# Expert rounds of a two-layer backbone: TensorE in the order of the text, and weights asked for in the order of their reading

## The chip, the cores and the metric

The kernel runs on one core of one Trainium2 chip. The metric is the device time of one execution in microseconds (us); of a kernel's runs the median counts. The profile is one execution recorded by the hardware profiler; its times are counted from the start of its span.

## What is computed

Two layers over 512 latent tokens of width 1024 and 256 context tokens. Each layer mixes tokens (three head groups and an output projection) and then sends the latent tokens, in the first layer the context tokens too, through 16 experts. In the second layer, the last, only the 512 latent tokens go through them. Each expert picks the 64 tokens that score highest for it:

```python
def expert_choice_moe(h, w_router, w_gate, w_up, w_down):
    b, n, d = h.shape
    cap = EC_FACTOR * n // N_EXPERTS
    aff = jax.nn.softmax(jnp.einsum('bnd,de->bne', h, w_router).astype(jnp.float32), axis=-1)
    g, idx = lax.top_k(jnp.swapaxes(aff, 1, 2), cap)
    xs = jax.vmap(lambda hb, ib: hb[ib])(h, idx)
    hid = jax.nn.silu(jnp.einsum('becd,edf->becf', xs, w_gate)) * jnp.einsum('becd,edf->becf', xs, w_up)
    y = jnp.einsum('becf,efd->becd', hid, w_down) * g[..., None].astype(h.dtype)
    return jax.vmap(lambda yb, ib: jnp.zeros((n, d), h.dtype).at[ib.reshape(-1)].add(yb.reshape(-1, d)))(y, idx)
```

## The kernel before

All of it is fp32. The change lies in the expert part of the second layer (`if last:` in `layer`, from line 1710). The 16 experts go in eight rounds p = 0 to 7 of two experts, 128 gathered token rows a round. A round has these steps; the letters are those of the strings `M1` and `TL`, which say in what order the Python text lists them:

- **p**, `prep`: GpSimd gathers the 128 rows from DRAM with two indirect DMAs (L1541).
- **t**, `prep_t`: TensorE transposes them in eight pieces (L1554) into two PSUM tiles B; ScalarE (L1205) and VectorE (L1207) scale four pieces each into the tile `xs`.
- **g**, `gu`: 32 matmuls with the gate and up weights into one PSUM tile A, eight pieces of the width times gate and up times two experts. The experts are i = 0, 1; each uses 64 columns of the array (128*64 in the trace), and i = 0 and i = 1 follow each other in turn. Then ScalarE's Silu (L1573) and VectorE's product (L1574).
- **h**, `th_`: four transposes of that product (L1594), and a copy by ScalarE (L143).
- **d**, `dn`: 16 matmuls with the down weights into a tile A, again i = 0, 1 in turn; VectorE scales it twice by halves (L1613), ScalarE copies it rounded into `yh` (L143, 128x1024), VectorE makes the rest `yl` (L146), and the one-hot `oh` of the token numbers (L1617).
- **s**, `scat`: for four blocks of 128 tokens and two halves of the width a full 128-column matmul of `oh` with `yh` and one with `yl` into a tile B, which VectorE adds to the residual (L1673).

In the trace each 64-column matmul has two records, while a transpose and a matmul with `yh` or `yl` has one. All PE matmuls of `mm` have line L155. There are two PSUM tiles A and four B.

The weights are 1 MB loads by the SP queue (`wload`, L137): eight for gate and up of a round (`loads_gu`), four for down (`loads_d`), into a pool of 18 pages `pg`, two of the four down loads into the two buffers `aw`. A load waits for its page's last reader and for the load four before it; the queue keeps its order, so whatever stands behind a waiting load waits too. The last round's down weights come as halves of the width, for `dn_half` and `scat_half`, which send the output.

The scheduler of the framework sets the order on each engine: it takes the instructions by priority and by its own account of when they are ready, so TensorE's order need not be that of the text.

The order of the text before is `M1 = "tghpsd"` in a round (for step p: transposes and gate/up of p+1, `th_` of p, gather of p+2, scatter of p-1, down of p) for p up to 5; at p = 6 only h, s and d. Then `TL = "tsgh0123"`: transposes of 7, scatter of 6, gate/up of 7, `th_` of 7, the two down halves and the two scatter halves. The loads stand ahead of each round:

```python
                if p < 5:
                    loads_gu(p + 2)
                    loads_d(p + 1)
                elif p == 5:
                    loads_d(6)
                    loads_gu(7)
                    loads_d(7)
```

Of the kernel before, what the change touches and what calls it, by code (L numbers as in the profile page):

```python
# [64 lines left out]
DO1 = 1  # L65
# [30 lines left out]
def tile_hybrid_dit(ctx: ExitStack, tc: tile.TileContext, I: dict, out: bass.AP, mark=lambda s: None):  # L96
# [107 lines left out]

# [1 line left out]
    def ada_load(l, hf, u, w):  # L206
# [229 lines left out]
    def layer(l):  # L436
# [6 lines left out]

# [1 line left out]
        mark("ln1")  # L445
# [216 lines left out]
        else:  # L662
            ht(0, 0)
            consts()
            for k in range(8):
# [7 lines left out]
                fill(FL1[0] if k in FL1[5] else 0)  # L673
# [1 line left out]
        rv, sv = small(8), small(8)  # L675
# [70 lines left out]
        early(0)  # L746
# [1 line left out]
        mark("G3")  # L748
# [3 lines left out]
        for j in range(npair):  # L752
# [6 lines left out]
            split(t.rearrange("p (z e) -> p z e", z=2), fhv[:, i:i + 2], flv[:, i:i + 2])  # L759
# [1 line left out]
        early(1)  # L761
# [58 lines left out]

# [1 line left out]
        mark("sgu")  # L822
# [24 lines left out]

# [1 line left out]
        mark("four")  # L849
# [46 lines left out]

# [1 line left out]
        if WM:  # L898
# [118 lines left out]

# [1 line left out]
        mark("kv")  # L1019
# [77 lines left out]

# [1 line left out]
        units = [(0, h, a) for h in range(4) for a in range(LT)]  # L1099
# [91 lines left out]

# [1 line left out]
        mark("wo")  # L1193
# [328 lines left out]
        def loads_gu(p):  # L1522
            if p < 8:
                mark("moe")
                wpages(("w_gate", "w_up"), p, 8, (6, 7) if p == 0 and AW0[l] else ())

        def loads_d(p):
            if p < 8:
                mark("moe")
                wpages(("w_down",), p, 4, (2, 3) if p or not AW0[l] else (), last and p == 7)  # L1530

# [1 line left out]
        xc2 = xc_d.rearrange("n (h d) -> (n h) d", h=2)  # L1533

        def prep(s, p):
            ig = R[s][1]
            xg = t4()
            if s == 0:
                for i in range(2):
                    e = 2 * p + i  # L1540
                    pool.indirect_dma_start(out=xg[64 * i:64 * i + 64], out_offset=None, in_=xr_d[0],  # L1541
                                            in_offset=bass.IndirectOffsetOnAxis(ap=ig[:, e:e + 1], axis=0))
            else:
                for i in range(4):
                    e = 2 * p + i
                    pool.indirect_dma_start(out=xg[32 * i:32 * i + 32], out_offset=None, in_=xr_d[1],
                                            in_offset=bass.IndirectOffsetOnAxis(ap=ig[0:32, e:e + 1], axis=0))
            M["xg", s, p] = xg

        def prep_t(s, p):  # L1550
            xg = M["xg", s, p]
            t = [psB(), psB()]
            for k in (0, 4, 1, 5, 2, 6, 3, 7):
                pe.transpose(t[k // 4][:, (k % 4) * 128:(k % 4 + 1) * 128], xg[:, k::8], ident)  # L1554
            xs = t4()
            modT(s, t, lambda k: xs[:, k * 128:(k + 1) * 128], 128)
            M["xs", s, p] = xs
            if s:
                M["xs", s, p + 1] = xs
# [150 lines left out]
        if last:  # L1710
            if not DO1:
                loads_d(0)
            prep(0, 0)
            prep(0, 1)
            prep_t(0, 0)
            gu(0, 0)
            for p in range(7):
                if p < 5:
                    loads_gu(p + 2)
                    loads_d(p + 1)  # L1720
                elif p == 5:
                    loads_d(6)
                    loads_gu(7)
                    loads_d(7)
                for o in M1:
                    if o == "t" and p < 6:
                        prep_t(0, p + 1)
                    elif o == "p" and p < 6:
                        prep(0, p + 2)
                    elif o == "g" and p < 6:  # L1730
                        gu(0, p + 1)
                    elif o == "h":
                        th_(0, p)
                    elif o == "d":
                        dn(0, p)
                    elif o == "s" and p:
                        scat(p - 1)
            for o in TL:
                if o == "t":
                    prep_t(0, 7)  # L1740
                elif o == "s":
                    scat(6)
                elif o == "a":
                    scat(6, (0, 1))
                elif o == "b":
                    scat(6, (2, 3))
                elif o == "g":
                    gu(0, 7)
                elif o == "h":
                    th_(0, 7)  # L1750
                elif o in "01":
                    dn_half(7, int(o))
                elif o in "23":
                    scat_half(7, int(o) - 2)
        else:
# [136 lines left out]
```

## Time and profile before

| what | value |
|---|---|
| median of 3 runs | 1277.88 us (1272.85 to 1279.33) |
| span of the profiled execution | 1275.3 us |
| TensorE busy in the span | 1167.6 us (92%) |
| VectorE, ScalarE, GpSimd busy | 579.9, 379.5, 301.3 us |
| mean granted TensorE clock | 0.963 |
| read from HBM | 295.01 MB, 240 GB/s over the span |

For the profiled execution only the span is given, from its first to its last instruction; the median of the runs lies 2.5 us above it, and the span lies within the runs' range. The expert part of the second layer is the last fifth of the span, from about 1009 us on. In the trace section a line of a timeline gives start, length, engine, line, operation, operands and count, and in brackets the idle time before it with what ended it. Lengths of TensorE rows have modelled ends and reach some 0.1 us into the next row.

### The profile page before, as it was taken

Reading aid. Unit: us, or ns where it says so; the run is one execution under the profiler, and the core shown is the slowest. Engines: PE = TensorE matmul, PEld = TensorE weight load, DVE = VectorE, ACT = ScalarE, POOL = GpSimd, SP = SyncE. Lnnn points to the kernel's source line nnn. Section 1 sums busy time; section 2 is a strip of 40 time slices with the busy share of each in tenths; the row PEclk is TensorE's granted clock in tenths of the full one; section 3 lists DMA queues with packets and bytes.
Section 4 is the critical chain, followed back from the end, with each engine's and each line's share of the span. In section 5 each row is a group of like instructions: output and inputs, shape, how many; then the busy total and the mean of one; then the engine's idle time right before and its main releaser. Section 6 shows DMA issues by size and latency. Waiting matters only on the chain. (4 is left out here: it accounts for less than half of the span.)

```text
span 1275.3 us, 16762 instructions
## 1 busy us (share of the span) xinstructions
PE 1167.6 (92%) x6440; PEld 664.5 (52%) x6440; DVE 579.9 (45%) x1219; ACT 379.5 (30%) x921; POOL 301.3 (24%) x363
## 2 busy tenths in 40 slices
PE   4999998999998999999999899999999399999887
PEld 2668865777763333333333378756776133333332
DVE  5634567666563133222333545767654503322352
ACT  4424466554222111101111234565542011101110
POOL 2413553222222212111100434742232200000000
PEclk8999997999998999999999899999999599999999
DMA  9871462013189999999986542550256799999593
GB/s 339 300 267 40 170 221 92 1 61 138 54 327 324 342 323 320 364 327 360 347 327 230 161 163 75 186 197 1 100 185 271 275 401 407 386 396 396 217 396 131
DMA packets 74319, 306.59 MB, mean 240 GB/s; under 512 B 11008, under 2 KB 20480, under 8 KB 46080
## 3 DMA queue, kind: packets, MB, share of 16 engines
q1 hardware_dynamic: 67328, 285.59, 59.8%
q0 software_dynamic: 6048, 17.83, 4.9%
q10 hardware_dynamic: 864, 2.10, 0.4%
q8 instruction: 51, 0.84, 0.3%
q14 instruction: 28, 0.23, 0.0%
HBM read 295.01 MB, written 10.49 MB: 240 GB/s over the span
## 5 line engine op out<-in xcount | busy, mean ns | idle before, releaser
L155 PE MATMUL A<-pg,pg 128*128 128x512 f32 (+4 forms) x1440 | 354.7, 389 | 13.6 <-DVE pg L146 4.6
L155 PE MATMUL A<-pg,t 128*64 128x512 f32 x1248 | 301.9, 607 | 7.3 <-ACT t L143 3.5
L155 PEld LDWEIGHTS A<-pg,pg 128*128 128x128 f32 (+1 forms) x1440 | 255.8, 192 | 82.0 <-issue 22.1
L155 PEld LDWEIGHTS A<-pg,t 128*64 128x64 f32 x1248 | 89.6, 139 | 184.8 <-issue 163.2
L155 PE MATMUL B<-t,t 128*128 128x512 f32 x256 | 74.8, 424 | 16.4 <-ACT t L143 14.4
L1673 DVE TENSOR_TENSOR pg<-pg,B 128x512 f32<-128x512 f32 x112 | 69.5, 681 | 41.8 <-PE B L155 41.6
L143 ACT ACTIVATE pg<-B 64x256 fp32r<-64x256 f32 (+6 forms) x153 | 65.0, 445 | 73.4 <-PE B L155 37.2
L146 DVE TENSOR_TENSOR pg<-B,pg 128x512 fp32r<-128x512 f32 (+4 forms) x143 | 69.9, 500 | 34.7 <-ACT pg L143 27.7
L155 PE MATMUL B<-pg,t 128*32 128x512 f32 (+1 forms) x672 | 82.5, 609 | 1.6 <-ACT t L143 1.2
L1541 POOL DMA_INDIRECT t<-xr_d,ig x32 | 29.2, 913 | 229.7 <-PE B L155 120.5
L155 PE MATMUL B<-pg,pg 128*128 128x256 f32 (+6 forms) x552 | 81.8, 302 | 0.1
L155 PEld LDWEIGHTS B<-pg,pg 128*128 128x128 f32 x552 | 73.9, 189 | 11.9 <-issue 5.9
L1573 ACT ACTIVATE t<-A 128x512 f32<-128x512 f32 x16 | 9.6, 597 | 235.4 <-PE A L155 235.4
L1574 DVE TENSOR_TENSOR t<-t,A 128x512 f32<-128x512 f32 x16 | 11.0, 686 | 147.8 <-ACT t L1573 147.8
L143 ACT ACTIVATE t<-B 128x512 f32<-128x512 f32 (+4 forms) x72 | 35.7, 496 | 135.0 <-PE B L155 49.0
L155 PEld LDWEIGHTS B<-t,t 128*128 128x128 f32 x256 | 43.8, 190 | 56.3 <-ACT t L143 18.4
L1613 DVE SCALAR_TENSOR_TENSOR A<-A,gc,pg 128x512 f32<-128x512 f32 x28 | 21.2, 759 | 87.6 <-PE A L155 87.1
L155 PE MATMUL A<-aw,t 128*64 128x512 f32 x224 | 60.8, 593 | 0.0
L1629 POOL DMA_INDIRECT xc_d<-t,isc x16 | 22.8, 1425 | 160.2 <-DVE t L1626 114.3
L1142 POOL TENSOR_SCALAR t<-t,s 128x768 f32<-128x768 f32 (+1 forms) x40 | 32.9, 822 | 98.7 <-DVE s L1141 91.6
L143 ACT ACTIVATE t<-A 128x1024 fp32r<-128x1024 f32 x14 | 14.3, 1023 | 133.9 <-DVE A L1613 84.6
L146 POOL TENSOR_TENSOR pg<-t,pg 128x512 fp32r<-128x512 f32 (+1 forms) x23 | 30.7, 1339 | 98.1 <-DVE t L569 50.3
(208 smaller groups left out, 1430.6 us busy)
## 6 DMA issues: line engine op xcount, KB each, us to landing
pg<-in_w_gate_dram SPq DMA_DIRECT2D x64, 1024.0 KB, 10.4
pg<-in_w_up_dram SPq DMA_DIRECT2D x62, 1024.0 KB, 9.9
pg<-in_w_down_dram SPq DMA_DIRECT2D x34, 1024.0 KB, 10.9
aw<-in_w_ada_dram SPq DMA_DIRECT2D x32, 1024.0 KB, 4.7
aw<-in_w_down_dram SPq DMA_DIRECT2D x30, 1024.0 KB, 8.2
pg<-in_w_ada_dram SPq DMA_DIRECT2D x16, 512.0 KB, 10.3
aw<-in_w_ada_dram SPq DMA_DIRECT2D x16, 512.0 KB, 4.9
pg<-in_w_out_dram SPq DMA_DIRECT2D x8, 1024.0 KB, 7.7
```

Of the source, the lines that this page charges most:

```text
L143: act.activation(o, i, AF.Copy, **k)
L146: eng.tensor_tensor(lo, full, f(hi), op=OP.subtract)
L155: lastmm[0] = pe.matmul(o, a, b, start=first, stop=last, skip_group_check=True)
L1142: pool.tensor_scalar(P[:, 0:W], P[:, 0:W], ri, 0.0, op0=OP.mult, op1=OP.add)
L1541: pool.indirect_dma_start(out=xg[64 * i:64 * i + 64], out_offset=None, in_=xr_d[0], in_offset=bass.IndirectOffsetOnAxis(ap=ig[:, e:e + 1], ...
L1573: act.activation(hd, t[:, 0:512], AF.Silu)
L1574: dve.tensor_tensor(hd, hd, t[:, 512:1024], op=OP.mult)
L1613: dve.scalar_tensor_tensor(t[:, hs], t[:, hs], gc[:, p:p + 1], gb[:, hs], op0=OP.mult, op1=OP.mult)
L1629: pool.indirect_dma_start(out=xc2, out_offset=bass.IndirectOffsetOnAxis(ap=sc[:, e:e + 1], axis=0), in_=y[64 * i:64 * i + 64], in_offset=N ...
L1673: dve.tensor_tensor(xa[:, hs], xa[:, hs], t, op=OP.add)
```

## The change

The branch of the last layer is written out as a plain loop, inside a block that takes TensorE's order from the text (the other engines keep the scheduler's). The strings `M1` and `TL` are not used there any more. Two things move in the text: round 6 now has its transposes and gate/up of round 7 ahead of `th_` of 6, scatter of 5 and down of 6, so these come before scatter of 6; and the loads of round 7's gate and up stand ahead of the down loads of 6, while the last down loads come one round later. The diff also takes out some comment lines.

```diff
         if last:
-            if not DO1:
-                loads_d(0)
-            prep(0, 0)
-            prep(0, 1)
-            prep_t(0, 0)
-            gu(0, 0)
-            for p in range(7):
-                if p < 5:
+            with tc.manual_schedule(engines={mybir.EngineType.PE}):
+                prep(0, 0)
+                prep(0, 1)
+                prep_t(0, 0)
+                gu(0, 0)
+                for p in range(7):
                     loads_gu(p + 2)
                     loads_d(p + 1)
-                elif p == 5:
-                    loads_d(6)
-                    loads_gu(7)
-                    loads_d(7)
-                for o in M1:
...
+                    prep_t(0, p + 1)
+                    gu(0, p + 1)
+                    th_(0, p)
+                    if p < 6:
                         prep(0, p + 2)
-                    elif o == "g" and p < 6:
-                        gu(0, p + 1)
-                    elif o == "h":
-                        th_(0, p)
-                    elif o == "d":
-                        dn(0, p)
-                    elif o == "s" and p:
+                    if p:
                         scat(p - 1)
-            for o in TL:
...
+                    dn(0, p)
+                th_(0, 7)
+                scat(6)
+                dn_half(7, 0)
+                dn_half(7, 1)
+                scat_half(7, 0)
+                scat_half(7, 1)
```

What this moves, first on TensorE in the middle of the part, before. Here A_8676 is gate/up of round 4, A_8754 down of round 3, B_8722 to B_8750 scatter of 2, B_8804 transposes of 5, B_8858 `th_` of 4:

```order
L155 MATMUL B_8722<-t_8625,t_8631 128x512
L155 MATMUL A_8676<-pg_8487,t_8667 64x512
L155 MATMUL A_8676<-pg_8489,t_8667 64x512
...
L155 MATMUL B_8722<-t_8626,t_8631 128x512
...
L155 MATMUL A_8676<-pg_8495,t_8667 64x512
L1554 MATMUL B_8804<-ident,t_8719 128x128 x3
L155 MATMUL A_8676<-pg_8497,t_8667 64x512
...
L155 MATMUL A_8754<-pg_8503,t_8717 64x512
L1594 MATMUL B_8858<-ident,t_8709 128x128 x4
L155 MATMUL A_8754<-pg_8505,t_8717 64x512
```

The same place after the change, where A_8678 is gate/up of 4, B_8714 `th_` of 3, B_8724 to B_8752 scatter of 2, A_8756 down of 3, B_8805 and B_8806 transposes of 5:

```order
L155 MATMUL A_8678<-pg_8503,t_8669 64x512
L1594 MATMUL B_8714<-ident,t_8565 128x128 x4
L155 MATMUL B_8724<-t_8627,t_8633 128x512
L155 MATMUL B_8724<-t_8628,t_8633 128x512
...
L155 MATMUL B_8752<-t_8628,t_8633 128x512
L155 MATMUL A_8756<-pg_8505,t_8719 64x512
L155 MATMUL A_8756<-pg_8507,t_8719 64x512
...
L155 MATMUL A_8756<-aw_8511,t_8719 64x512
L1554 MATMUL B_8805<-ident,t_8721 128x128
```

Each step now stands whole: the transposes no longer part a pair of gate/up matmuls, `th_` of 4 no longer the first pair of down, and scatter of 2 comes behind all of gate/up 4 rather than around a quarter of it.

Next TensorE at the end, before: A_9194 is gate/up of 7, B_9162 and the like scatter of 6, A_9118 down of 6, B_9144 the last of round 7's transposes.

```order
L155 MATMUL A_9118<-aw_8931,t_9084 64x512
L1554 MATMUL B_9144<-ident,t_9019 128x128
...
L155 MATMUL B_9166<-t_9135,t_9141 128x512
L155 MATMUL A_9194<-pg_8933,t_9153 64x512
L155 MATMUL B_9162<-t_9136,t_9141 128x512
...
L155 MATMUL A_9194<-pg_8935,t_9153 64x512
L155 MATMUL A_9194<-pg_8933,t_9153 64x512
L155 MATMUL B_9174<-t_9135,t_9141 128x512
```

After the change: A_9175 is down of 6, B_9200 `th_` of 7, B_9207 to B_9235 scatter of 6, B_9239 the first down half of 7. Gate/up of 7 stands before all of this.

```order
L155 MATMUL A_9175<-aw_8949,t_9141 64x512
L1594 MATMUL B_9200<-ident,t_9133 128x128 x4
L155 MATMUL B_9207<-t_9192,t_9198 128x512
L155 MATMUL B_9207<-t_9193,t_9198 128x512
...
L155 MATMUL B_9235<-t_9193,t_9198 128x512
L155 MATMUL B_9239<-pg_9073,t_9205 64x512
```

So behind down of 6 stand scatter of 6 and the last round's down alone, with gate/up of 7 no longer between them.

Last the SP queue, before: aw_8801 ends the loads of down 5, pg_8925 to aw_8931 are down 6, pg_8933 and what follows gate/up 7.

```order
L137 DMA aw_8801<-in_w_down_dram 128x2048
L137 DMA pg_8925<-in_w_down_dram 128x2048
L137 DMA pg_8927<-in_w_down_dram 128x2048
L137 DMA aw_8929<-in_w_down_dram 128x2048
L137 DMA aw_8931<-in_w_down_dram 128x2048
L137 DMA pg_8933<-in_w_gate_dram 128x2048
```

After the change: aw_8803 ends down 5, pg_8927 to pg_8941 are gate/up 7, pg_8943 to aw_8949 down 6, pg_9073 begins down 7.

```order
L137 DMA aw_8803<-in_w_down_dram 128x2048
L137 DMA pg_8927<-in_w_gate_dram 128x2048
...
L137 DMA pg_8941<-in_w_up_dram 128x2048
L137 DMA pg_8943<-in_w_down_dram 128x2048
...
L137 DMA aw_8949<-in_w_down_dram 128x2048
L137 DMA pg_9073<-in_w_down_dram 128x4x512
```

The eight loads of gate/up 7 no longer stand behind the two `aw` loads of down 6, which wait until down of 5 has read those buffers.

VectorE's, ScalarE's and GpSimd's instructions are the same in number; on ScalarE the copy to `yh` still stands ahead of the four L1205 of the next transposes, and on VectorE the L146 for `yl` ahead of the four L1207.

## Rows read from the trace of the kernel before

**Rows 1.** Expert part: length; PE, PEld, DVE, ACT, POOL busy; granted clock, DMA share, GB/s.

```profile
1009.43:1270.57 261.14, 237.36 (x992) 90.58 (x992) 78.74 (x135) 29.93 (x58) 10.35 (x12) 0.96 0.85 334
```

**Rows 2.** Timeline of TensorE, rounds 0 to 2.

```profile
1029.68 13.95 PE L155 MATMUL A<-pg,t 128*64 128x512 f32 x64 [1.30 <-ACT t L1205]
...
1045.06 7.09 PE L155 MATMUL A<-pg,t 128*64 128x512 f32 x32
...
1055.02 0.50 PE L155 MATMUL B<-t,t 128*128 128x512 f32 x1 [1.98 <-ACT t L143]
1055.45 15.65 PE L155 MATMUL A<-pg,t 128*64 128x512 f32 x64
```

**Rows 3.** Timeline of TensorE, rounds 2 to 6.

```profile
1083.04 1.16 PE L1554 MATMUL B<-ident,t 128*128 128x128 f32 x8
...
1112.23 1.16 PE L1554 MATMUL B<-ident,t 128*128 128x128 f32 x8
...
1119.07 4.40 PE L155 MATMUL B<-t,t 128*128 128x512 f32 x15
...
1137.46 1.07 PE L155 MATMUL A<-pg,t 128*64 128x512 f32 x2 [1.18 <-ACT t L143]
...
1148.97 0.49 PE L155 MATMUL B<-t,t 128*128 128x512 f32 x1 [2.75 <-ACT t L143]
...
1182.13 5.35 PE L155 MATMUL A<-pg,t 128*64 128x512 f32 x16
...
1214.96 1.20 PE L155 MATMUL B<-t,t 128*128 128x512 f32 x4 [2.75 <-ACT t L143]
```

**Rows 4.** Timeline of TensorE, from the end of down 6 on.

```profile
1228.56 1.05 PE L1554 MATMUL B<-ident,t 128*128 128x128 f32 x7
1231.42 0.73 PE L155 MATMUL B<-t,t 128*128 128x512 f32 x2 [1.80 <-ACT t L143]
...
1254.03 5.27 PE L155 MATMUL B<-pg,t 128*64 128x512 f32 x16 [0.69 <-ACT t L143]
...
1262.01 0.70 PE L155 MATMUL B<-t,t 128*128 128x512 f32 x2 [1.85 <-DVE t L1647]
```

**Rows 5.** Last line of the chain that ended last: start, us, engine, operand, line.

```profile
1271.35 0.60 DVE pg L1659
```

**Rows 6.** Groups of instructions by form, expert part: count, busy us, mean ns, idle before.

```profile
L1673 DVE TENSOR_TENSOR pg<-pg,B 128x512 f32<-128x512 f32 x56 | 34.6, 681 | 38.4 <-PE B L155 38.4
...
L1205 ACT ACTIVATE t<-B,mod 128x128 f32<-128x128 f32 x32 | 12.0, 462 | 21.3 <-issue 21.3
...
L1613 DVE SCALAR_TENSOR_TENSOR A<-A,gc,pg 128x512 f32<-128x512 f32 x14 | 10.6, 759 | 48.8 <-PE A L155 48.6
...
L146 DVE TENSOR_TENSOR t<-A,t 128x1024 fp32r<-128x1024 f32 x7 | 8.6, 1225 | 8.1 <-ACT t L143 8.1
L143 ACT ACTIVATE t<-A 128x1024 fp32r<-128x1024 f32 x7 | 7.2, 1023 | 78.5 <-DVE A L1613 45.0 <-issue 21.0 <-PE B L1554 12.6
```

**Rows 7.** Busy time by stretch, stretches at the lower clock; columns as in rows 1.

```profile
1182.24:1185.65 3.41, 3.41 (x10) 0.97 (x12) 1.95 (x5) 0.81 (x3) 0.00 (x0) 0.50 1.02 420
1216.37:1219.78 3.41, 3.41 (x10) 1.18 (x6) 1.19 (x2) 0.00 (x0) 0.00 (x0) 0.50 1.02 425
...
721.44:731.68 10.24, 9.23 (x28) 4.14 (x27) 4.36 (x6) 2.11 (x3) 3.49 (x4) 0.50 0.73 245
```

**Rows 8.** Timeline of the SP queue around the loads of round 7.

```profile
1185.82 2.82 SPq L137 DMA_DIRECT2D pg<-in_w_down_dram  x2
1211.40 1.17 SPq L137 DMA_DIRECT2D aw<-in_w_down_dram  x2
1212.62 0.93 SPq L137 DMA_DIRECT2D pg<-in_w_gate_dram  x2
```

**Rows 9.** Busy time by stretch, eight gate/up loads running; columns as in rows 1.

```profile
1086.78:1106.70 19.92, 19.92 (x89) 7.71 (x87) 7.52 (x15) 1.54 (x4) 1.06 (x2) 1.00 1.01 420
```

**Rows 10.** DMA issues of the whole span: count, KB each, median us from issue to landing.

```profile
pg<-in_w_gate_dram SPq DMA_DIRECT2D x64, 1024.0 KB, 10.4
```

More of the change, by code (lines that the diff above doesn't have):

```diff
@@ L1710, in layer @@
         if last:
-            if not DO1:
-                loads_d(0)
-            prep(0, 0)
-            prep(0, 1)
-            prep_t(0, 0)
-            gu(0, 0)
-            for p in range(7):
-                if p < 5:
+            with tc.manual_schedule(engines={mybir.EngineType.PE}):
[4 more added lines that the diff above has]
+                for p in range(7):
                     loads_gu(p + 2)
                     loads_d(p + 1)
-                elif p == 5:
-                    loads_d(6)
-                    loads_gu(7)
-                    loads_d(7)
-                for o in M1:
-                    if o == "t" and p < 6:
-                        prep_t(0, p + 1)
-                    elif o == "p" and p < 6:
-                        prep(0, p + 2)
-                    elif o == "g" and p < 6:
-                        gu(0, p + 1)
-                    elif o == "h":
-                        th_(0, p)
-                    elif o == "d":
-                        dn(0, p)
-                    elif o == "s" and p:
-                        scat(p - 1)
-            for o in TL:
[L1739 to L1754, printed above, removed]
+                    prep_t(0, p + 1)
+                    gu(0, p + 1)
+                    th_(0, p)
+                    if p < 6:
+                        prep(0, p + 2)
+                    if p:
+                        scat(p - 1)
+                    dn(0, p)
[5 more added lines that the diff above has]
+                scat_half(7, 1)
         else:
```

## The prediction

> **What bounds the kernel now.** I read the busy time by stretch first, for the part that the change touches. From the first transposes of round 0 to the last matmul, 261.1 us, TensorE is busy for 237.4 and idle for 23.8, more than any other engine; the 16 DMA engines have a share of 0.85 [rows 1]. So the part is near both limits, and the timeline of TensorE has to say which of them is met where. I write t(p), gu(p), th(p), sc(p), dn(p) for round p's transposes, gate/up, `th_`, scatter and down, and E(p) for the end of dn(p).
>
> The timeline of TensorE never shows an idle time that ends with a weight load. It ends with ScalarE's copies, in two sorts. One of 2.75 us comes when sc(p) stands next behind dn(p): the copy to `yh` needs dn(p)'s result, scaled twice by VectorE, 2 x 0.759, and then copied, 1.023, which with the handovers makes the 2.75 [rows 3, 6]. One of 1.2 us comes ahead of dn, which waits for a copy that ScalarE has behind the Silu of a gate/up just ended [rows 3]. From these rows: E(1) = 1083.0 and E(2) = 1112.2, where the next transposes begin; E(3) = 1148.97 - 2.75 = 1146.2; E(5) = 1214.96 - 2.75 = 1212.2 [rows 3]; E(6) = 1228.6 [rows 4]. So rounds 4 and 5 take 33.0 us each, and after E(6) the last add ends at 1271.35 + 0.60 = 1271.95, 43.4 later [rows 5], because gu(7) is still to come.
>
> Beside idle time there is work that takes longer than it must. Whole, gu takes 13.95 us and dn 7.09 [rows 2]. In the order before, th parts dn's first pair of matmuls: the first of the two, alone, takes 1.07 [rows 3], as long as a pair otherwise needs with its partner in the other half of the array (13.95 for 16 pairs is 0.87 a pair, rows 2). So a parted pair costs about 1.0, and dn(1) to dn(5) have one each.
>
> **The change, part by part.** *Order in a round.* Now it is t(p+1), gu(p+1), th(p), sc(p-1), dn(p). Behind E(p), t(p+2) runs at once (1.16, rows 3). Then gu(p+2) needs `xs`, whose first piece ScalarE makes only behind the copy to `yh`: 2.75 and one L1205 of 0.46, so it starts at E + 3.2 [rows 3, 6]. The idle time is 3.2 - 1.1 = 2.1, the only one left in a round: sc(p-1) needs a `yh` made a whole gu earlier, and th's copy lies under sc. The removed waits are thus 2.75 + 1.2, the added one 2.1. VectorE's pieces of `xs` come behind `yl`, so from E + 2.75 + 1.23 = 3.98 on [rows 6], but gu reads the first of them with its fifth pair, 3.5 us after its start, so they cost nothing. Sc fills a tile in 2 x 0.29 and VectorE empties one in 0.681 [rows 3, 6]: over eight tiles it falls some 0.9 us behind, which four buffers take; without them that 0.9 would be added to each round.
>
> A round, each row less the 0.1 by which it reaches into the next: 3.2 + 13.9 + th 0.65 (my estimate from the four transposes among the eight of 1.16) + 16 x 0.288 = 4.6 + 7.0 = **29.4 us** [rows 2, 3]. Dn(0) cannot start sooner than now, at 1045.06, as its copy waits for th(0); E(0) stays 1052.1, gu(2) starts at 1055.3 against 1055.45 now, with the same slow stretch behind it [rows 2], and then 0.65 + 4.6 + 7.0 bring E(1) to 1083, as now. Five rounds more: E(6) = 1083.0 + 5 x 29.4 = 1230.0. That is the E(6) of before, 1.4 later, but with gu(7) done.
>
> *Tail.* Behind E(6): th(7); `yh` at 2.75, and the first matmul of sc(6); the second waits for `yl`, 1.23 more, so at 3.98; 15 x 0.288 to 8.3; the two halves of dn(7), 7.0, to 15.3. What VectorE has left then is one scaling, 0.76, eight adds of 0.68 and one `yl`, 0.6 to 0.7: 6.9, so the last add ends at E(6) + 22.2 = 1252.2, against 1271.95. Sc(7)'s matmuls, 16 x 0.288, lie under that. The last add is followed by 3.4 us to the end of the span today (1275.3 - 1271.95), so the span is **1255.6** at the full clock.
>
> *Loads.* Before, the queue pauses from 1188.6 to 1211.4, for an `aw` buffer that dn(5) still reads, with gu(7)'s weights behind it, which are first asked for at 1212.6 [rows 8]. In the new order gu(7) starts at E(5) + 3.2 = 1203.8, so with the old order of loads its last pages, eight loads behind 1212.6 at 2.5 us each, would come over 20 us after its start; the moved loads earn nothing by themselves but carry the whole tail. Loads run at 420 GB/s [rows 9], so a round's twelve of 1 MB [rows 10] take 30.0 us, 0.6 more than a round of TensorE. Is that enough lead? The `aw` loads of dn(2) go out at E(1); then gu(4)'s eight. Its sixth page goes out at 1083 + 7 x 2.5 = 1100.5 and lands 10.4 later [rows 10], 1110.9; gu(4) starts at 1115.6 and reads it from the fifth pair on, 1119. The lead is 8 us and shrinks by 0.6 a round, to 6 at gu(7). The pause itself moves behind gu(7): the last `aw` loads wait for E(6), land some 10.4 later and are needed at 8.3 + 3.5 = 11.8. Gathers still stand a round ahead.
>
> *Clock.* This is the unknown term. Four of the part's waits were followed by a stretch at the lower clock (1.2 GHz instead of 2.4): those that end at 1055.02 (gu 15.65 for 13.95), before 1182.13, at 1214.96 and at 1254.03 (5.27 for half a dn); the ones that end at 1148.97, 1231.42 and 1262.01 were not, though 1.8 to 2.75 us long [rows 2 to 4, 7]. Such a stretch lasts 3.41 us at a granted 0.50 [rows 7] and costs half of that, 1.7, as 15.65 against 13.95 shows [rows 2]. The new order has six waits behind E(1): five of 2.1 and the tail's of 2 and 1. Between 0 and 6 x 1.7 = 10.2 I take three, by the four of seven: 5.1.
>
> The Trainium skill (TensorE: Matmul & The Clock Gate, section "A second HAM failure mode: psum-queue depth-cycling") speaks against this order: short idle times that recur between groups of matmuls make the clock swing between its levels, and the way back is paid between the bursts. Taken for every wait, the sum would have 10.2 in place of 5.1. The trace agrees in part, with four of seven.
>
> *Sum.* 1255.6 + 5.1 = 1260.7, against 1275.3. The runs' median lies 2.5 above the span; so **1263 us**, 14.6 less: the last add comes 19.7 earlier, and 5.1 of that go to the clock.
>
> **Rivals.** *Weights late.* Now TensorE reads gu(7) 10 us and more earlier. If loads keep their present pace of some 33 us a round, of which 30.0 are transfer, the lead of 8 shrinks by 3.6 a round, is gone at gu(6), and gu(7) and dn(6) wait for 3 to 9: 1266 to 1272. For it: share 1.01, no room to catch up [rows 9]. Against: the pauses were waits for buffers that dn read late, and dn is now earlier.
>
> *Clock lost in every wait:* 1255.6 + 10.2 + 2.5 = 1268. For it: the same wait recurs in each round. Against: [rows 3], where 2.75 idle passed without. It is what the skill's rule above gives.
>
> *No gain:* what TensorE no longer waits for it waits for at gu, as its first piece hangs on the copy to `yh`, the very copy of before. If gu had to wait for all eight pieces, with `yl` and VectorE's four ahead (3.98, and four at ScalarE's 12.0 / 32 = 0.375, rows 6), it would start at E + 5.5, 2.3 later in five rounds, and with the clock lost each time: 1255.6 + 11.5 + 10.2 + 2.5 = 1280. For it: VectorE's order. Against: the 1.30 ahead of gu(1), ended by an L1205 [rows 2], is less than four pieces of 0.375 on one engine.
>
> *Slower:* the clock, once lost between dn and gu, stays low for longer than 3.41. The longest low stretch of a busy part lasts 10.24 [rows 7], costing 5.1; six of these are 30.7: 1255.6 + 30.7 + 2.5 = 1289. It decides from 3.7 us lost a wait, 7.4 us low, where the 22 gained are used up. Against: in [rows 2, 3] the stretch ends while gu is running.
>
> *The change does less than it says:* the other engines keep the scheduler's order; if a copy of ScalarE stood behind a later Silu as before, 1.2 a round would stay, 6 in all: 1269. The order as built shows none.
>
> **How the numbers follow.** A measurement of this kernel can tell some 0.5% from no change, 6.4 us, here 1271.5. The forecast has 0.70, clock lost in every wait 0.09, weights late 0.10, less than it says 0.03, no gain 0.05, slower 0.03. Faster takes the first four, less a little of late weights: 0.90; same 0.07; slower 0.03. The range goes from no loss of clock, 1255.6 + 2.5 less a us of rounding, 1257, to the middle of late weights and above the lost clock, 1270.
>
> **What would show it.** Right: rounds of 29 to 31 us, one idle time of 2.0 to 2.2 in each, ended by ScalarE's L1205 ahead of gu; dn whole in 7.0 us; gu(7) ahead of dn(6); last add 22 us behind E(6); an SP pause only ahead of the last two loads. Wrong: idle times of TensorE that end with a load, gu starting more than 4 us behind dn, low clock over 3.41 us in a round, or E(6) later than 1240.

## The result, and the profile after

The changed kernel takes 1257.7 us (median of 4 runs, 1256.18 to 1259.7) against 1277.88 before: a ratio of 0.9857, interval 0.9827 to 0.9886. (The ratio on record, here and in the table below, is not taken from the two medians, which give 0.984.) The forecast was 1263 in a range of 1257 to 1270, so the result lies at the range's lower end. The profiled run, the slowest of the four, took 1259.7 us, with a span of 1257.8.

In the busy time by stretch, from the first transposes to the last add (columns as in [rows 1]), the part lasts 245.06 us; before, the stretch 1009.43:1271.95 was 262.52. So all of the gain, 17.5 us, lies in it.

```profile
1009.24:1254.30 245.06, 225.77 (x992) 91.54 (x992) 79.58 (x137) 30.46 (x58) 10.36 (x12) 0.95 0.92 358
```

TensorE's timeline of the changed kernel, one round (E(1) to E(2)), the start of each later one, and the start of the tail:

```profile
1081.82 1.16 PE L1554 MATMUL B<-ident,t 128*128 128x128 f32 x8
1085.05 15.65 PE L155 MATMUL A<-pg,t 128*64 128x512 f32 x64 [2.08 <-ACT t L1205]
1100.63 0.75 PE L1594 MATMUL B<-ident,t 128*128 128x128 f32 x4
1101.14 4.12 PE L155 MATMUL B<-t,t 128*128 128x512 f32 x16
1105.18 3.65 PE L155 MATMUL A<-pg,t 128*64 128x512 f32 x16
1108.66 3.60 PE L155 MATMUL A<-aw,t 128*64 128x512 f32 x16
1112.20 1.16 PE L1554 MATMUL B<-ident,t 128*128 128x128 f32 x8
...
1142.55 1.16 PE L1554 MATMUL B<-ident,t 128*128 128x128 f32 x8
...
1172.90 1.16 PE L1554 MATMUL B<-ident,t 128*128 128x128 f32 x8
1176.11 13.95 PE L155 MATMUL A<-pg,t 128*64 128x512 f32 x64 [2.05 <-ACT t L1205]
...
1201.56 1.16 PE L1554 MATMUL B<-ident,t 128*128 128x128 f32 x8
1204.76 15.65 PE L155 MATMUL A<-pg,t 128*64 128x512 f32 x64 [2.05 <-ACT t L1205]
...
1231.90 0.74 PE L1594 MATMUL B<-ident,t 128*128 128x128 f32 x4
1234.71 0.50 PE L155 MATMUL B<-t,t 128*128 128x512 f32 x1 [2.06 <-ACT t L143]
1235.97 5.13 PE L155 MATMUL B<-t,t 128*128 128x512 f32 x15 [0.76 <-DVE t L146]
```

The waits of 2.75 and 1.2 us and the parted pairs of [rows 3] are gone; one wait of 2.05 to 2.1 a round stands in their place, ended by ScalarE's L1205. A round takes 30.35 us where the clock falls behind that wait (gate/up 15.65) and 28.66 where it doesn't (E(4) = 1172.90 to E(5) = 1201.56). E(6) is 1231.90, and the last line of VectorE's timeline ends at 1254.30, 22.4 later:

```profile
1250.63 3.67 DVE L1659 TENSOR_TENSOR pg<-pg,B 128x512 f32<-128x512 f32 x6
```

The clock, from stretches as in [rows 7]: two of the six at half clock behind E(1), the gate/up between them that kept the full clock, then two of three rounds of loads, each from one issue of gate's second half to the next:

```profile
1085.46:1088.87 3.41, 3.41 (x10) 0.98 (x8) 2.12 (x6) 0.59 (x2) 0.00 (x0) 0.50 1.00 407
...
1176.11:1189.99 13.88, 13.88 (x64) 4.50 (x64) 2.52 (x6) 0.99 (x3) 0.00 (x0) 1.00 1.01 420
1204.92:1208.33 3.41, 3.41 (x10) 0.99 (x10) 2.37 (x6) 0.83 (x3) 0.00 (x0) 0.50 1.01 420
...
1096.60:1129.60 33.00, 30.95 (x139) 12.20 (x136) 9.88 (x17) 3.61 (x7) 1.78 (x2) 0.95 1.02 395
...
1162.70:1195.80 33.10, 31.05 (x144) 13.45 (x144) 14.33 (x26) 3.64 (x8) 1.77 (x2) 1.00 1.02 395
```

Five of the six waits behind E(1) were followed by such a stretch, all but the one before 1176.11. And a round of loads took 33.0 to 33.1 us, not 30, at 395 GB/s, in each of the three rounds, all with a gather (POOL's two records, 1.78). The SP queue shows the same pace, and two pauses for the `aw` buffers: one of 5.9 us ahead of 1081.91, which ends with down of 1, and one of 13.2 us ahead of 1231.99, which ends with down of 6. The prediction named only the second as a sign of being right; the first was there before, too, ahead of 1082.30:

```profile
1073.15 2.82 SPq L137 DMA_DIRECT2D pg<-in_w_down_dram  x2
1081.91 0.88 SPq L137 DMA_DIRECT2D aw<-in_w_down_dram  x2
...
1096.63 2.86 SPq L137 DMA_DIRECT2D pg<-in_w_gate_dram  x2
...
1195.84 2.87 SPq L137 DMA_DIRECT2D pg<-in_w_gate_dram  x2
...
1215.76 3.03 SPq L137 DMA_DIRECT2D pg<-in_w_down_dram  x2
1231.99 1.22 SPq L137 DMA_DIRECT2D aw<-in_w_down_dram  x2
```

Of the two loads from 1195.84 on, the second goes out at 1198.4; the loads of this stretch land 9.9 us behind their issue (median), so it lands at 1208.3. Gate/up 7 reads it from its fifth pair on, 3.5 us (5.2 with the low clock) after 1204.76, at 1208.3 to 1210. The weights were just in time.

### The profile page after: what moved, and what is told of

The parts are those of the page before. It is cut to its first block, busy times and chain, and to the rows that moved or that the text cites. A ratio compares the mean times of both kernels' runs of the same rounds, so it can differ in the third digit from the quotient of the medians.

```text
span 1257.8 us, 16770 instructions
## 1 busy us (share of the span) xinstructions
PE 1155.7 (92%) x6440; PEld 664.5 (53%) x6440; DVE 580.3 (46%) x1219; ACT 379.6 (30%) x921; POOL 300.5 (24%) x363
## 4 chain that ended last, share of the span: by engine, by line
PE 79%; DVE 7%; DMA 6%; ACT 3%; issue 3%; POOL 2%; SPq 0%; DVEq 0%; ACTq 0%; POOLq 0%
PE A L155 48%; PE B L155 24%; PE B L1154 2%; DMA pg<-in_w_ada_dram 2%; DMA aw<-in_w_ada_dram 1%; DVE pg L146 1%; PE B L1594 1%; PE B L1554 1%; ACT pg L143 1%; DMA pg<-in_ctxT_dram 1%; DVE A L1613 1%; DVE t L1351 1%; PE B L1304 1%; DMA pg<-in_rowp_dram 1%; DVE t L1350 1%
## 5 line engine op out<-in xcount | busy, mean ns | idle before, releaser
L155 PE MATMUL A<-pg,t 128*64 128x512 f32 x1248 | 297.2, 616 | 15.4 <-ACT t L1205 14.1
L155 PEld LDWEIGHTS A<-pg,pg 128*128 128x128 f32 (+1 forms) x1440 | 254.2, 191 | 82.9 <-issue 21.6
L146 DVE TENSOR_TENSOR pg<-B,pg 128x512 fp32r<-128x512 f32 (+4 forms) x143 | 70.0, 500 | 33.9 <-ACT pg L143 27.0
L1573 ACT ACTIVATE t<-A 128x512 f32<-128x512 f32 x16 | 9.6, 597 | 217.6 <-PE A L155 205.1
L155 PE MATMUL B<-t,t 128*128 128x512 f32 x256 | 70.6, 417 | 2.9 <-ACT t L143 2.1
L155 PE MATMUL A<-aw,t 128*64 128x512 f32 x224 | 55.5, 592 | 0.0
L146 POOL TENSOR_TENSOR pg<-t,pg 128x512 fp32r<-128x512 f32 (+1 forms) x23 | 30.2, 1317 | 98.6 <-DVE t L569 46.3
L155 PE MATMUL B<-aw,cT 128*32 128x512 f32 (+1 forms) x384 | 50.3, 540 | 2.6 <-DMA aw<-in_w_ada_dram 2.6
```

Of the source, the lines that this page charges most:

```text
L146: eng.tensor_tensor(lo, full, f(hi), op=OP.subtract)
L155: lastmm[0] = pe.matmul(o, a, b, start=first, stop=last, skip_group_check=True)
```

## The experiments

These kernels do the same work up to the expert part, yet in their profiles its first transposes start anywhere from 1001.57 to 1012.26 us. So small effects are read from the **part**: from the start of the first transposes to the end of the last add, and from E(6) on. The part comes from one profile of each kernel; the two profiles of the changed kernel (changed, after_again) differ by 1.2 us in it. All on one core; third_less and no_gather have two runs each; the kernel before had medians of 1274.56, 1275.15 and 1273.72 on the three chips of these runs. Where gate/up 7 stands behind down 6 (before, rounds_only, loads_alone), the last column contains it.

| kernel | median | ratio to before, interval | part | behind E(6) |
|---|---|---|---|---|
| before | 1277.88 | - | 262.5 | 43.4 |
| changed | 1257.7 | 0.9857 (0.9827 to 0.9886) | 245.1 | 22.4 |
| rounds_only | 1261.72 | 0.9890 (0.9839 to 0.9940) | 248.8 | 39.4 |
| text_sched | 1270.77 | 0.9966 (0.9939 to 0.9994) | 258.3 | 21.6 |
| order_old_loads | 1275.36 | 0.9995 (0.9969 to 1.0020) | 261.6 | 22.6 |
| loads_alone | 1271.54 | 0.9981 (0.9954 to 1.0007) | 258.3 | 40.3 |
| yh_late | 1256.23 | 0.9834 (0.9789 to 0.9879) | 241.9 | 21.1 |
| fill_wait | 1258.17 | 0.9848 (0.9801 to 0.9895) | 245.0 | 22.3 |
| tail | 1253.08 | 0.9837 (0.9788 to 0.9887) | 243.3 | 19.8 |
| combo | 1250.22 | 0.9818 (0.9766 to 0.9870) | 237.7 | 19.8 |
| third_less | 1235.86 | 0.9703 (0.9659 to 0.9748) | 226.5 | 21.1 |
| no_gather | 1234.39 | 0.9692 (0.9648 to 0.9735) | 224.9 | 19.8 |
| after_again | 1254.07 | 0.9837 (0.9809 to 0.9865) | 246.3 | 22.6 |
| combo_again | 1253.27 | 0.9815 (0.9774 to 0.9857) | 238.0 | 19.8 |

### Which part of the change earns it

**rounds_only** keeps gate/up 7 behind down 6, and the old order of loads:

```diff
-                    prep_t(0, p + 1)
-                    gu(0, p + 1)
+                    if p < 6:
+                        prep_t(0, p + 1)
+                        gu(0, p + 1)
...
-                th_(0, 7)
+                prep_t(0, 7)
                 scat(6)
+                gu(0, 7)
+                th_(0, 7)
```

> TensorE in the order of the text, but round 7's gate/up stays behind down of 6 as before, and the loads in the old order. Theory: the order inside the rounds earns most of it. E(5) comes at 1202 as in the changed kernel, 10.6 us ahead of before; then round 6 without a gate/up takes th 0.5, a wait of 2, scatter 4 and down 7, some 15, and from E(6) the last add follows 43.4 us later as before: about 1262 to 1266 us. Rival 1, the rounds only hand their waits to the clock and the gain lies in gate/up 7 alone: no more than 3 us below the kernel before. Rival 2, the moved loads carry all: as before, 1278.

E(5) came at 1201.42, E(6) at 1217.85. The part is 13.7 us shorter than before: E(6) comes 209.4 us behind the first transposes, before 219.1, and what follows it took 39.4 rather than 43.4. Gate/up 7 isn't the reason for that: `th_` of 7 starts 24.75 us behind E(6), before 24.0. The gain lies behind it. Before, the first half of down 7 ran in part at half clock, and a scatter matmul that waited 1.85 us parted the second half [rows 4]; here the two halves stand side by side at the full clock. From the start of down 7 to the last add it is 13.26 us, before 17.92. First the lines of before that [rows 4] leave out, then rounds_only:

```profile
1259.13 1.02 PE L155 MATMUL B<-aw,t 128*64 128x512 f32 x2
...
1262.64 3.65 PE L155 MATMUL B<-aw,t 128*64 128x512 f32 x14
```

```profile
1217.85 1.16 PE L1554 MATMUL B<-ident,t 128*128 128x128 f32 x8
...
1242.60 0.74 PE L1594 MATMUL B<-ident,t 128*128 128x128 f32 x4 [1.42 <-DVE t L1574]
1244.03 3.65 PE L155 MATMUL B<-pg,t 128*64 128x512 f32 x16 [0.69 <-ACT t L143]
1247.51 3.60 PE L155 MATMUL B<-aw,t 128*64 128x512 f32 x16
```

**text_sched** is the changed kernel without the block that gives TensorE the text's order:

```diff
-            with tc.manual_schedule(engines={mybir.EngineType.PE}):
-                prep(0, 0)
+            prep(0, 0)
...
```

> The text and the loads of the changed kernel, but the scheduler sets TensorE's order: gate/up 7 stands ahead of down 6, while inside the rounds the transposes still part gate/up, th_ parts down's first pair, and scatter stands where it stood. Theory: rounds of 33 us up to E(6), some 1244 to 1245, and the tail of 22.4 us of the changed kernel behind it, 1270 to 1273 us, 5 to 8 below before. Rival 1, the gain is gate/up 7's place: 1258 as the changed kernel. Rival 2, the loads of round 7 wait for down of 5 anyway: 1278.

As expected: E(6) at 1245.4, the last add 21.6 later, and the old 2.75 and 1.19 in each round:

```profile
1248.20 5.68 PE L155 MATMUL B<-t,t 128*128 128x512 f32 x16 [2.76 <-ACT t L143]
```

The part is 4.2 shorter than before. It looks as if the two runs added up (13.7 + 4.2 = 17.9, together 17.5), but both contain the same gain at the end. In text_sched down 7 starts 245.0 us behind the first transposes, before 244.6, and from there it is 13.27 us, as in rounds_only. So under the scheduler's order gate/up 7's place earned nothing, and the 4.2 are down 7's two halves.

Read by stretch, the 17.5 us are three parts. Up to the start of down 7 it is 244.6 us before, 235.6 in rounds_only and 231.8 in the changed kernel: some 9.0 for the order inside the rounds, and 3.8 for gate/up 7's place (2.6 against after_again), which pays only together with that order. The last 4.65 lie behind the start of down 7. The order inside the rounds is the largest part and stands well clear of the 1.2 us between profiles; the 3.8 rests on one profile of rounds_only, and the intervals of its ratio and the changed kernel's overlap.

**order_old_loads** and **loads_alone** take the loads apart from the order. The first puts the old three lines for p = 5 back into the changed loop, the second puts the new loads into the kernel before:

```diff
-                    loads_gu(p + 2)
-                    loads_d(p + 1)
+                    if p < 5:
+                        loads_gu(p + 2)
+                        loads_d(p + 1)
+                    elif p == 5:
+                        loads_d(6)
+                        loads_gu(7)
+                        loads_d(7)
```

> The changed order of TensorE with the old order of loads (down 6 ahead of gate/up 7). Theory: the first load of gate/up 7 is issued only when down of 5 has read its aw buffers, at about 1203; the eighth lands some 23 us later, at 1226, so gate/up 7 ends near 1229.5 instead of 1220.3, with waits of TensorE that end with loads: 9 us above the changed kernel, 1266 to 1270 us. Rival, pages are free early enough and the order of loads is indifferent: 1258.

> The kernel before with the new order of loads alone (gate/up 7 ahead of down 6, down 7 a round later). Theory: no wait of TensorE before ended with a load, so nothing is gained: 1275 to 1280 us, E(5) at 1212. Rival, weights asked for in the order of reading are worth something by themselves: 1265 to 1272.

The first lost not 9 us but 16.5, nearly the whole gain (part 261.6). E(5) is 1197.98 there, and gate/up 7 waits for loads four times:

```profile
1208.13 1.94 PE L155 MATMUL A<-pg,t 128*64 128x512 f32 x2 [8.99 <-DMA pg<-in_w_gate_dram]
1210.53 4.14 PE L155 MATMUL A<-pg,t 128*64 128x512 f32 x14 [0.46 <-DMA pg<-in_w_gate_dram]
1218.10 1.67 PE L155 MATMUL A<-pg,t 128*64 128x512 f32 x2 [3.43 <-DMA pg<-in_w_gate_dram]
1220.49 12.84 PE L155 MATMUL A<-pg,t 128*64 128x512 f32 x46 [0.72 <-DMA pg<-in_w_gate_dram]
...
1198.08 0.81 SPq L137 DMA_DIRECT2D aw<-in_w_down_dram  x2
1198.93 1.22 SPq L137 DMA_DIRECT2D pg<-in_w_gate_dram  x2
```

My estimate had taken the landing of the eighth load as the limit. It is the fifth and sixth: they hold the second half of gate's rows, which gate/up reads ahead of anything of up, and three quarters of the step still stand behind them, here in part at half clock (12.84 us where the same 46 records take 10.51 in yh_late). The eighth load was also put too early: it went out at 1215.5 and, with 10 us to landing, came 27.5 us behind E(5), not 24. This is not what the order of loads is worth by itself, but what it costs to move gate/up 7 without it: rounds_only has the old order of loads, too, and a part of 248.8.

The loads alone gave 0.9981 with an interval that includes 1: no wait of before ended with a load. The part did come out 4.2 us shorter in the one profile, and it is the same gain again: with the new order of loads the scheduler put down 7's halves side by side, which I had not allowed for. Down 7 starts 245.0 us behind the first transposes, and from there it is 13.27 us:

```profile
1250.65 3.65 PE L155 MATMUL B<-pg,t 128*64 128x512 f32 x16 [0.69 <-ACT t L143]
1254.14 3.60 PE L155 MATMUL B<-aw,t 128*64 128x512 f32 x16
```

### What the clock and the wait cost

**fill_wait** puts two matmuls into the wait; their result isn't read:

```diff
                     prep_t(0, p + 1)
+                    if p:
+                        w = psB()
+                        for _ in range(2):
+                            mm(w, ident, gb[:, 0:512], True, True)
```

> The changed kernel with two added fp32 matmuls (128x512, into a tile that nobody reads) behind the transposes of each round, where TensorE waits 2.05 us for xs. Theory: they fit into the wait and cost nothing, and the low clock that follows that idle time is gone: no stretch at 0.50 behind E(0) to E(5), gate/up 13.95 in every round, a round 28.7 us where loads allow it; gain 3 to 6 us, 1252 to 1255. Rival 1, the clock falls by something else than that idle time: still five of six stretches, 1258. Rival 2, the added matmuls don't fit: each round 1 us or more longer, 1262 and above.

```profile
1112.72 1.88 PE L155 MATMUL B<-pg,ident 128*128 128x512 f32 x4
1114.94 13.95 PE L155 MATMUL A<-pg,t 128*64 128x512 f32 x64 [0.33 <-ACT t L1205]
...
1173.19 3.65 PE L155 MATMUL A<-pg,t 128*64 128x512 f32 x16 [0.33 <-ACT t L1205]
1178.88 1.04 PE L155 MATMUL A<-pg,t 128*64 128x512 f32 x2 [2.03 <-DMA pg<-in_w_gate_dram]
1181.27 13.48 PE L155 MATMUL A<-pg,t 128*64 128x512 f32 x46 [1.35 <-DMA pg<-in_w_gate_dram]
...
1057.60:1169.98 112.38, 111.36 (x500) 44.76 (x500) 37.65 (x66) 13.06 (x26) 7.12 (x8) 1.00 1.02 396
```

The mechanism was right: with 0.33 us left of the wait no stretch at half clock follows, and the four rounds from E(0) to E(4) run at a granted 1.00. The gain was not: the part is 245.0, as in the changed kernel. In gate/up 5 TensorE has used up the loads' lead (14.91 us for 13.95, with 0.8 in which a load of weights into the array waits for gate); in gate/up 6 it waits 2.03 and 1.35 and loses the clock there, for 6.83 us. That the part comes out equal to 0.1 us is in part chance, since this half clock lengthens what is left of gate/up 6 to 13.48 us where 10.51 would do.

**yh_late** takes the wait away at its root:

```diff
-                copy(yh, t)
-                sub(dve, yl, t, yh)
...
+                def post():
+                    yh, yl = t4(F32R), t4(F32R)
+                    copy(yh, t)
+                    sub(dve, yl, t, yh)
...
                     prep_t(0, p + 1)
+                    if p:
+                        M["post", p - 1]()
```

> The changed kernel with one thing moved: the copies of down's result (yh, yl) are written behind the next transposes, so ScalarE makes the first pieces of xs ahead of yh. Theory: the 2.05 us wait behind each down hangs on that copy; it falls to some 0.7 (one L1205 of 0.46 and handovers), and with it most of the low clock, as the 0.75 us ahead of down 0 cost none. A round of TensorE is then 27.3 us, less than a round of loads (29.8 at 420 GB/s, about 33 with its gathers), so the last rounds begin to wait for loads: TensorE idle times that end with DMA, and only some 5 us of gain: 1250 to 1254 us. Rival 1, loads don't bind: 6 x 1.35 and 5 x 1.7 less, 1241. Rival 2, loads or another engine set the rounds already: 1258 as the changed kernel.

```profile
1055.35 13.95 PE L155 MATMUL A<-pg,t 128*64 128x512 f32 x64 [0.48 <-ACT t L1205]
...
1137.80 3.65 PE L155 MATMUL A<-pg,t 128*64 128x512 f32 x16 [0.44 <-ACT t L1205]
1144.91 1.04 PE L155 MATMUL A<-pg,t 128*64 128x512 f32 x2 [3.46 <-DMA pg<-in_w_gate_dram]
1147.30 13.21 PE L155 MATMUL A<-pg,t 128*64 128x512 f32 x46 [1.35 <-DMA pg<-in_w_gate_dram]
```

The wait falls to 0.43 to 0.49 and the first rounds to 27.1; from gate/up 4 on TensorE waits for gate's fifth and sixth load, 8.7 us in all. The part gains 3.2 (1.3 of it in the tail, which keeps the full clock here), less than the 5 expected, and far from the 16.6 of the rival in which loads don't bind.

### What sets the rounds next

**third_less** drops loads from yh_late:

```diff
+                    if last and kt == 8 and z and p > 2:
+                        for k in range(kk):
+                            Wt[name, p, i, kk + k] = Wt[name, p, i, k]
+                        continue
                     g = awp() if c in aw else page()
```

> The kernel with the late yh, but from round 3 on the second half of gate's and up's rows isn't loaded, and the first half's weights stand in for it: four of twelve loads a round are left out of the computation, TensorE's work stays. Theory: loads set the pace of the last four rounds there (29.9 to 35.8 us where TensorE has 27.1 of work and wait). With eight loads, some 20 us and the gather, every round comes at 27.1: E(6) 42.3 + 6 x 27.1 = 204.9 us behind the first transposes instead of 220.8, the last add 21 later, 1240 us. No idle time that ends with DMA, no stretch at half clock in the rounds. Rival, something other than loads (the half clock itself, an engine) sets those rounds: 1254 to 1256.

E(6) came 205.4 us behind the first transposes, where 204.9 were expected; every round takes 27.0 to 27.1, no idle time in the rounds ends with DMA, and from 1011.95 to the last add the granted clock is 1.00. So it was the loads.

```profile
1211.01 0.75 PE L1598 MATMUL B<-ident,t 128*128 128x128 f32 x4
...
1011.95:1232.14 220.19, 210.90 (x976) 85.85 (x972) 77.87 (x133) 28.95 (x54) 9.02 (x10) 1.00 0.78 300
```

**tail** moves the first half of down 7 ahead of scatter 6 and lets its last loads go into pages:

```diff
-                wpages(("w_down",), p, 4, (2, 3) if p or not AW0[l] else (), last and p == 7)
+                wpages(("w_down",), p, 4, (2, 3) if (p or not AW0[l]) and not (last and p == 7) else (), last and p == 7)
...
                 th_(0, 7)
-                scat(6)
                 dn_half(7, 0)
+                scat(6)
                 dn_half(7, 1)
```

> The changed kernel with another tail: the first half of down 7 stands ahead of scatter 6, and all four loads of down 7 go into pages, so that none waits for down of 6. Theory: the wait of 2.06 and 0.76 us behind th of 7 is covered by that half, a wait of some 0.9 for th's copy stays, and from E(6) the last add follows 19 to 20 us later instead of 22.4: 1255 us. Rival, VectorE sets the tail (16 us of work from E(6) on and its waits): 22 us from E(6) as now, 1258.

From E(6) on 19.8 us instead of 22.4, by the mechanism named: the wait is 0.69, for th's copy. Half of the 2.6 is the clock, which is not lost behind this wait: at the full clock the old tail takes 21.1 (yh_late).

```profile
1226.46 3.65 PE L155 MATMUL B<-pg,t 128*64 128x512 f32 x16 [0.69 <-ACT t L143]
```

**combo** joins yh_late and tail, and asks for gate's four pages before up's:

```diff
...
+            if last and kt == 8:
+                zn = [(z, name, i) for name in names for z in range(2) for i in range(2)]
...
```

> The late yh and the other tail together, and gate's four loads of a round asked for ahead of up's four, which is the order in which gate/up reads them. Theory: the gains add, and the loads that a round needs first come 5 us earlier, so that the lead lasts longer: E(6) 6 to 8 us earlier than in the changed kernel, the tail 2 to 3 shorter, 1246 to 1250 us. Rival 1, loads set the pace by their sum whatever their order: 1251 to 1254. Rival 2, no gain: 1258.

> The changed kernel once more, beside the next on one chip: 1254 to 1260 us, from the first transposes to the last add 245 us; of the waits behind each down again most, not all, followed by a stretch at half clock.

> The three edits together (late yh, other tail, gate's loads first) once more, on the same chip as the changed kernel. Theory: 238 us from the first transposes to the last add instead of 245, so 7 us below the changed kernel, 1247 to 1252. Rival, the earlier median was the chance of its runs: within 2 us of the changed kernel.

The changed kernel came out as before (1254.07, and five of its six waits ahead of gate/up 2 to 7 lost the clock). The parts are 237.7 and 238.0 against 245.1 and 246.3 of the changed kernel: 7 to 8 us, twice, the tail's 2.6 and some 5 up to E(6), where 6 to 8 were expected. The medians on one chip, 1253.27 and 1254.07, don't tell the two apart: the combo's six runs lie between 1240.87 and 1256.02, its ratio to before is 0.9815 against 0.9837, with intervals that overlap, and in the profiles its part began 5.6 us later (1010.23 against 1004.61). So it is faster where it was changed; by the whole time that is not shown.

**no_gather** asks what makes a round of loads 33 us:

```diff
-            if s == 0:
+            if last and p > 2:
+                pool.memset(xg, 0.5)
+            elif s == 0:
```

> The kernel with the late yh, the other tail and gate's loads first, in which the token rows of rounds 3 to 7 aren't gathered: GpSimd fills the tile with a constant, so the computation leaves those tokens out. Theory: the gathers cost the loads some 3 us a round (a round of loads lasts 33.1 us with one and 29.9 without), four of them in the stretch where loads never pause; without them the loads of gate/up 7 come 13 us sooner and TensorE's 13.7 us of waits in gate/up 5 to 7 go, or nearly: E(6) 204 to 207 us behind the first transposes instead of 217.9, 1237 to 1240 us. Rival, the 3 us come from the wait for the aw buffers, which falls at the same point of the round: no change, 1250.

E(6) is 205.1 behind the first transposes, with no wait for a load in the rounds, as in third_less. The stretches, first combo with a gather and without one, then E(6) and a stretch of no_gather:

```profile
1146.30:1179.40 33.10, 28.68 (x126) 11.28 (x124) 9.88 (x17) 3.62 (x7) 1.78 (x2) 1.00 1.01 396
1179.40:1209.20 29.80, 27.83 (x126) 11.25 (x124) 9.87 (x17) 3.62 (x7) 0.00 (x0) 1.00 1.01 421
```

```profile
1210.80 0.74 PE L1599 MATMUL B<-ident,t 128*128 128x128 f32 x4
...
1072.80:1102.60 29.80, 29.30 (x138) 11.65 (x134) 9.88 (x17) 3.62 (x7) 0.95 (x1) 1.00 1.01 419
```

Without gathers twelve loads take 29.8 us in the three rounds from 1043.0 to 1132.4, also in the one shown, in which `aw` loads wait for down of 1. So a gather costs some 3.3 us, and the rival with the `aw` buffers falls.

## Why the prediction was right, and where it was not

*Order in a round, and what it removes:* right. The wait forecast at 2.1 was 2.05 to 2.13 and hung on the copy to `yh`, as yh_late shows by moving that copy; down is whole again (from 1105.18 to 1112.20, 7.0); rounds_only puts the order's share at some 9 of 17.5 us.

*A round of 29.4:* 0.74 too long. At the full clock it is 28.66: scatter takes 4.04 rather than 4.6, as 0.25 a matmul, not the 0.288 of [rows 3]; th adds 0.5, not 0.65. Why scatter is quicker when it stands whole wasn't tried; in the row at 1119.07 [rows 3] its loads into the array wait five times for VectorE's adds, 1.5 us in all, at 1101.14 of the changed kernel twice, 0.5. Five rounds, 3.7.

*Up to E(1):* forecast 1083.0, found 1081.82; 0.7 of it was already there at E(0) (1051.38 against 1052.1), the rest is scatter 0.

*Tail:* 22.2 forecast, 22.4 measured, but with half clock in it. At the full clock it is 21.1 (yh_late, third_less).

*Clock:* mis-sized. Three of six waits at 1.7 were taken; five came, four of them in the rounds (6.8) and one in the tail (22.4 - 21.1 = 1.3): 8.1 for 5.1. The four of seven that the term went by were waits of unlike length, 0.69 to 2.75. In the five profiles that have the wait of 2.05 to 2.14 behind down ahead of gate/up, 23 of 28 such waits were followed by a stretch at half clock (gate/up 15.65 for 13.95); where it was 0.33 to 0.50 (fill_wait, yh_late, both combos, third_less, no_gather), none of 36 was by itself; in fill_wait and yh_late the clock fell once each, behind waits for loads. The Trainium skill (TensorE: Matmul & The Clock Gate, "A second HAM failure mode: psum-queue depth-cycling") says that short idle times which recur between groups of matmuls make the clock swing. These traces agree with it, more than [rows 3, 7] did.

*Sum:* the span forecast was 1260.7: less 1.2, 3.7 and 1.1, plus 3.0 for the clock and 0.1 at the end, 1257.8, as measured. The 2.5 added to reach the median were mis-sized by 0.6: each of the four runs lies 1.8 to 1.9 above its own span. But the profiled run is 2.0 above the median, so the median lies 0.1 below the profiled span. That is scatter of the runs, as a span moves with the start of the part, by 10 us between profiles. How near 1263 came is thus in part luck: terms 6.0 too long, one 3.0 too short.

*Loads:* this step was wrong, though nothing came of it. That a round's twelve take 30.0 us was worked out from [rows 9], a stretch of eight loads at whose end a gather is only just issued; with the gather it is 33.1. The reason given against *weights late*, that the 33 were waits for buffers, falls with no_gather. The lead was not 6 us at gate/up 7 but 0 to 1.7. That it lasted at all is luck of two kinds. It began higher: the sixth page for gate/up 4 was read 21.4 us behind its issue (1099.2 to 1120.6), not 18.5. And while the premise of the rival *weights late* held (loads at 33 a round), its waits didn't come, because the low clock stretched TensorE's rounds to 30.35. Clock and loads were summed up as if apart; here the larger of the two counted, and fill_wait shows it: without the low clock in four rounds the part lasts as long. That the rivals' prices did not add is what I had not seen.

*No idle time of TensorE ending with a load, the load order carrying the tail:* right, and by more than forecast (order_old_loads gives back 16.5 of the 17.5 us).

*The rival "slower":* its turning point was taken from 22 us of gain. By the sum the gain at the full clock is 19.7 (1275.3 - 1255.6), so it lies at 3.3 us lost a wait, 6.6 us low. The stretches in the rounds stayed at 3.41.

## What to carry to other kernels

When a wait is taken out of a loop, work out next to it the pace of the resource that comes second, with everything that shares it, here the gathers, and how many rounds its lead lasts; beyond that point further gains on the first resource are worth little (fill_wait nothing; yh_late 3.2 us, where 16.6 were to be had without that second limit). When two trial kernels seem to add up to the whole, compare them stretch by stretch: here both held the same 4.65 us at the end. In the same loop, a copy that is needed a round later should be written behind the copies that are needed now. The order in which loads are asked for should be checked against the order of reading down to the single page: it decides which page is late.

## What the runs showed of the hardware

A gather of 128 rows (0.52 MB, two indirect DMAs) cost the running loads 3.3 us, where 0.52 MB at 420 GB/s would be 1.25. In combo's round 1146.3 to 1179.4 its packets hold the 16 DMA engines for 5.6% of 33.1 us, 1.9 us; the rest of the loss isn't explained here. The Trainium skill (DMA: Bandwidth & Descriptors, "Issuing engines are not separate DMA queues") says that transfers started by different engines run on the same 16 DMA engines and interleave. The rate of 396 against 420 GB/s, at a DMA share of 1.01 in both, agrees.

Idle times of 2.05 to 2.14 us, one a round, were followed by half clock in 23 of 28 cases (for 3.41 us in each of the changed kernel's five), and those of 0.33 to 0.50 us in none; fill_wait shows that it is the idle time, as filling it keeps the clock. What spares the other five isn't settled. Nor is what moves the start of the expert part by 10 us between profiles, and by 4.6 between the two of the changed kernel.
